# Loads of the next tile's keys and values issued a step ahead in a gated-delta recurrence, with their gate products behind the state sums

## The chip, the cores and the metric

The kernel runs on one core of a Trainium2 chip, in one launch. The metric is the device time of one execution in microseconds (us). Five engines work from queues of their own, each in the order in which its instructions stand: TensorE (PE, matmuls; its weight loads are shown as PEld), VectorE (DVE), ScalarE (ACT), GpSimd (POOL) and SyncE (SP). Transfers between the device's memory (DRAM) and the core's memory are issued from the queues of SP and ACT (shown as SPq and ACTq).

## The reference

A latent of 512 tokens by 1024 goes through two blocks beside a context of 256 tokens, all in float32. The change touches the first block's bidirectional gated-delta recurrence:

```
def gated_delta_chunked(q, k, v, g_log, beta, s0):
    # 8 heads of 64, chunks of 64 tokens
    ...
    w_mat = triangular_solve(t_mat, (bc * eG)[..., None] * kc, ...)
    u_v = triangular_solve(t_mat, bc[..., None] * vc, ...)
    k_tail = jnp.exp(g_last[..., None] - G)[..., None] * kc
    def step(S, xs):
        w_c, uv_c, qd_c, intra_c, kt_c, gl_c = xs
        u = uv_c - einsum('bhck,bhkv->bhcv', w_c, S)
        o = einsum('bhck,bhkv->bhcv', qd_c, S) + einsum('bhij,bhjv->bhiv', intra_c, u)
        S = exp(gl_c)[..., None, None] * S + einsum('bhck,bhcv->bhkv', kt_c, u)
        return S, o
```

It runs forwards and backwards, first over the context and then, from the states that this leaves, over the latent. `t_mat` is a triangular matrix of keys and gates for each chunk. The second block (two layers of attention, pooling and MLP) and the final norm aren't touched.

## The kernel before

The recurrence is `delta()`. Keys and values of the 768 tokens lie in DRAM as six tiles of 128 tokens by 512 (8 heads of 64), which makes 256 KB each. A **step** `s` (0 to 5) takes one tile for each direction `d`; steps 0 and 1 are the context, 2 to 5 the latent. A tile holds two chunks, which are the two **halves** `i` of a step. The steps go in three **groups** of two, and a group has three stages:

- `subst(g)` inverts 32x32 blocks of the triangular matrices on VectorE. A block copy on ScalarE (L959) and a transpose `Lw` (L960) come first, then 31 rounds of a product (L967) and a subtraction (L969), each needing the one before.
- `merges(g)` makes 64x64 inverses of them: two transposes on VectorE (L984 makes `Z2`, L985 `Z1`), matmuls (L993, L1003, L1006), and copies into the group's matrix on ScalarE (L1011 copies `Z2` and `Z1`, four instructions each; L997, L1014) and VectorE (L1015). The group's matrices take the buffer `M` that the stage before read.
- `chains(g)` carries the states through the two steps. A step makes `WT` from the gated keys `kb` (L1046 on PE, copied by ACT L1049), then `U` from the gated values `vc` (L1059). For each half, `U` takes up the state (L1072), ScalarE copies it to `u` (L1078), PE forms the state products `d` from the keys `kc` (L1092), and VectorE adds them to the decayed state (the **state sums**, L1102; the decay `Sg`, L1083). From step 2 on the outputs follow (L1112, L1116, copied by L1119 or summed by L1121), and for steps 4 and 5 `output()` (L1132 loads `sz`).

`fetch(s, d)` brings a tile: two loads that ScalarE's queue issues (L1027 keys, L1028 values) and at once the three gate products on VectorE (L1030, 128x512 each): `kb` is the keys by one gate, `vc` and `kc` are scaled in place. There are two buffers of each for each direction. Step `s+1` is fetched inside step `s`, once its `WT` stands, between the matmuls of `U`.

The group's substitution and merges run beside the chains of the group before it: `side_by_side` interleaves the generators and `weave` fills in work that doesn't depend on them. One filler is `attn_half()`, eight rounds of a weight load (L724, SP) that is split in two (ACT L728 `whi`, DVE L729 `wlo`), a gate load (L726, SP) for ACT's sigmoid (L730 `ga`), 12 matmuls (L447), a product on VectorE (L738) and a store from ScalarE's queue (L739). Its buffer `wst` is single. The other is `ada()`: weight loads on SP (L193) and matmuls (L201). These are interleaved as the code says, and then a scheduler in the compiler fixes the order on each engine (`schedule_with_timeline_sim=True`), so that a moved line can move others too.

## Time and profile before

| what | value |
|---|---|
| device time, median of 3 runs | 2660.58 us (2660.32, 2660.58, 2667.91) |
| the profiled execution's own time | 2655.62 us |
| its span (first to last instruction) | 2653.8 us |
| mean granted TensorE clock | 0.958 of full |
| instructions | 40142 |
| busy: TensorE, VectorE, ScalarE, GpSimd | 2469.4, 1486.5, 1004.2, 875.8 us |

The span is one execution as the hardware profiler saw it; 1.8 us of that execution lie outside it. The recurrence takes some 206 of the span's 2653.8 us, from about 456 to 662 us after its start. Times below are counted from the span's start. "Idle before" is how long an engine did nothing ahead of an instruction, with what ended that; the name behind it is inferred from semaphores.

### The profile page before, as it was taken

The numbers are of one execution on the slowest core, as the hardware profiler recorded it, in microseconds if no ns is written. First come the engines' busy times: TensorE is split into PE (matmuls) and PEld (weight loads), VectorE is DVE, ScalarE is ACT, GpSimd is POOL, SyncE is SP. The second block draws the span as 40 slices with busy tenths as digits, with TensorE's granted clock in tenths as the row PEclk, the third lists the DMA queues.
The fourth block names the chain that finished last, engine by engine and source line by source line (L and its number), as shares of the span: only waits on it lengthen the run. The fifth ranks groups of instructions, "written<-read, shape, count | busy, mean of one in ns | idle before, by whom it ended". The sixth has DMA issues, their size and how long they took to land.

```text
span 2653.8 us, 40142 instructions
## 1 busy us (share of the span) xinstructions
PE 2469.4 (93%) x16082; PEld 2097.0 (79%) x16082; DVE 1486.5 (56%) x2532; ACT 1004.2 (38%) x1824; POOL 875.8 (33%) x719
## 2 busy tenths in 40 slices
PE   6897997878999899999998999999998999999998
PEld 3886776556877778799787888888887987888888
DVE  4557658775479942352784887676227357522225
ACT  4545453432442232342663413121224265522332
POOL 2443101000742332455334523232235523523331
PEclk7998998788999999999999999999999999999999
DMA  7231164664535533310012253433212101233331
GB/s 258 74 101 44 56 188 153 219 221 163 179 107 183 167 119 99 100 63 25 9 52 92 94 159 117 126 125 116 64 64 66 44 17 64 85 97 99 96 106 48
DMA packets 249145, 282.53 MB, mean 106 GB/s; under 512 B 12168, under 2 KB 207359, under 8 KB 248703
## 3 DMA queue, kind: packets, MB, share of 16 engines
q1 hardware_dynamic: 225582, 249.86, 29.6%
q10 hardware_dynamic: 23376, 30.11, 3.4%
q8 instruction: 126, 2.06, 0.3%
q14 instruction: 61, 0.49, 0.1%
HBM read 264.06 MB, written 15.88 MB: 105 GB/s over the span
## 4 chain that ended last, share of the span: by engine, by line
PE 70%; DVE 15%; DMA 6%; ACT 4%; issue 3%; POOL 1%; SPq 0%; ACTq 0%; POOLq 0%; DVEq 0%
PE mm L447 60%; DMA wada<-in_w_ada_dram 3%; DVE aacc L242 2%; DVE nt L313 2%; PE sc L1825 2%; PE mm L1850 1%; DVE wlo L108 1%; PE mm L1859 1%; PE mm L1354 1%; DVE tmp L967 1%; ACT whi L435 1%; DVE X L969 1%; DMA ga<-sga 1%; DMA Gb<-grows 1%; PE mm L201 0%
## 5 line engine op out<-in xcount | busy, mean ns | idle before, releaser
L108 POOL TENSOR_TENSOR wlo<-wst,whi 128x1024 fp32r<-128x1024 f32 (+2 forms) x141 | 367.2, 2605 | 769.7 <-ACT whi L435 753.6
L435 ACT ACTIVATE whi<-wst 128x1024 fp32r<-128x1024 f32 (+2 forms) x293 | 287.9, 1031 | 636.4 <-PE mm L447 350.5
L447 PE MATMUL mm<-hmxl,whi 128*128 128x512 f32 (+1 forms) x816 | 314.3, 387 | 4.1 <-DVE hmxl L316 3.2
L447 PE MATMUL mm<-hmxh,whi 128*128 128x512 f32 (+1 forms) x816 | 310.8, 386 | 6.7 <-ACT hmxh L315 6.3
L447 PE MATMUL mm<-hmxh,wlo 128*128 128x512 f32 (+1 forms) x816 | 312.5, 385 | 2.5 <-DVE wlo L108 2.5
L447 PE MATMUL mm<-hidxl,whi 128*128 128x512 f32 (+1 forms) x720 | 280.6, 390 | 7.0 <-DVE hidxl L1478 7.0
L447 PE MATMUL mm<-hidxh,wlo 128*128 128x512 f32 (+1 forms) x720 | 279.9, 389 | 2.4 <-DVE wlo L108 2.4
L447 PE MATMUL mm<-hidxh,whi 128*128 128x512 f32 (+1 forms) x720 | 277.4, 388 | 0.0
L108 DVE TENSOR_TENSOR wlo<-wst,whi 128x1024 fp32r<-128x1024 f32 (+1 forms) x152 | 193.2, 1276 | 148.0 <-ACT whi L435 147.8
L242 DVE SCALAR_TENSOR_TENSOR aacc<-wada,silu,aacc 128x512 f32<-128x512 f32 x280 | 249.0, 937 | 26.0 <-DMA wada<-in_w_ada_dram 25.6
L329 DVE SCALAR_TENSOR_TENSOR xres<-mm,mod,xres 128x512 f32<-128x512 f32 (+1 forms) x122 | 85.0, 703 | 235.9 <-PE mm L447 235.7
L1474 POOL TENSOR_TENSOR nsq<-nt 128x512 f32<-128x512 f32 (+1 forms) x134 | 138.2, 1033 | 149.2 <-ACT nt L1473 127.7
L447 PEld LDWEIGHTS mm<-hmxh,whi 128*128 128x128 f32 x816 | 156.5, 194 | 37.3 <-ACT hmxh L315 7.3
L447 PEld LDWEIGHTS mm<-hmxl,whi 128*128 128x128 f32 x816 | 157.5, 193 | 35.5 <-DVE hmxl L316 4.8
L447 PEld LDWEIGHTS mm<-hmxh,wlo 128*128 128x128 f32 x816 | 157.5, 193 | 33.5 <-DVE wlo L108 3.7
L1478 DVE TENSOR_TENSOR hidxl<-nsq,hidxh 128x512 fp32r<-128x512 f32 (+1 forms) x102 | 75.8, 744 | 172.1 <-POOL nsq L1474 170.6
L447 PEld LDWEIGHTS mm<-hidxl,whi 128*128 128x128 f32 x720 | 136.2, 189 | 37.0 <-DVE hidxl L1478 9.4
L447 PEld LDWEIGHTS mm<-hidxh,wlo 128*128 128x128 f32 x720 | 136.1, 189 | 31.4 <-DVE wlo L108 3.2
L447 PEld LDWEIGHTS mm<-hidxh,whi 128*128 128x128 f32 x720 | 136.0, 189 | 27.8
L1473 ACT ACTIVATE nt<-mm 128x512 f32<-128x512 f32 (+1 forms) x134 | 69.5, 520 | 230.7 <-PE mm L447 224.7
L447 PE MATMUL mm<-whi,h2xh 128*128 128x256 f32 x384 | 110.4, 290 | 3.9 <-ACT raw L1608 2.6
L447 PE MATMUL mm<-wlo,h2xh 128*128 128x256 f32 x384 | 109.2, 287 | 0.0
(517 smaller groups left out, 6033.6 us busy)
## 6 DMA issues: line engine op xcount, KB each, us to landing
wst<-in_w_mlp_dram SPq DMA_DIRECT2D x96, 1024.0 KB, 5.5
wada<-in_w_ada_dram SPq DMA_DIRECT2D x160, 256.0 KB, 2.7
wst<-in_w_in_dram SPq DMA_DIRECT2D x35, 1024.0 KB, 5.4
wada<-in_w_ada_dram SPq DMA_DIRECT2D x48, 512.0 KB, 5.3
wst<-in_w_out_dram SPq DMA_DIRECT2D x10, 1024.0 KB, 7.0
wada<-in_w_ada_dram SPq DMA_DIRECT2D x8, 1024.0 KB, 13.7
xacc<-in_w_out_dram SPq DMA_DIRECT2D x16, 256.0 KB, 2.9
Gb<-grows SPq DMA_DIRECT2D x12, 256.0 KB, 4.2
```

The lines of the kernel that those rows point to most:

```text
L108: e.tensor_tensor(out, x, hi.bitcast(F32), ALU.subtract)
L242: nc.vector.scalar_tensor_tensor(acc[j], wt, c, acc[j], ALU.mult, ALU.add)
L313: nc.vector.scalar_tensor_tensor(t, x[:, k, :], a(k), self.rb[n], ALU.mult, ALU.mult)
L329: nc.vector.scalar_tensor_tensor(x[:, m, :], ps[:, :T], gate(m, n), x[:, m, :], ALU.mult, ALU.add)
L435: self.nc.scalar.activation(hi[:, :, c0:c1], st[:, :, c0:c1], AF.Copy)
L447: self.nc.tensor.matmul(ps, lhs[a](k), rhs[b](k), start=first and i == 0, stop=last and i == n - 1)
L967: nc.vector.tensor_tensor(t, Lw[:, j + 1:, j:j + 1].to_broadcast([P, n, w]), x[:, j:j + 1, 0:w].to_broadcast([P, n, w]), ALU.mult)
L969: nc.vector.tensor_tensor(x[:, j + 1:, 0:w], x[:, j + 1:, 0:w], t, ALU.subtract)
L1473: nc.scalar.activation(t, ps[:, :T], AF.Relu)
L1474: nc.gpsimd.tensor_tensor(s2, t, t, ALU.mult)
L1478: self.latest = nc.vector.tensor_tensor(lo, s2, hi.bitcast(F32), ALU.subtract)
L1825: mm = nc.tensor.matmul(ps[:, c0:c1], QT_[:, w, t * P:(t + 1) * P], KT_[:, c0:c1], start=w == 0, stop=w == 1)
```

## The change

`fetch` is split. It now only issues the two loads, and is called for step `s+1` at the start of step `s`, ahead of `WT`. A new `scale(s, d)` does the three gate products: for a group's first step ahead of the loop, and for step `s+1` direction by direction behind the state sums of the two halves of step `s`. No instruction is added or taken away on any engine. Line numbers behind this place grow by 7 to 11: the product is L1037, `WT` L1060, the `u` copy L1088, `Sg` L1093, the state sum L1112, the `oacc` copy L1130.

```diff
                 k, v, kb = (self.T(pool, [P, 8, CH], f"{n}{d}", bufs=2) for n in ("kc", "vc", "kb"))
                 nc.scalar.dma_start(out=k.rearrange("p h f -> p (h f)"), in_=tokd["k"][t])
                 nc.scalar.dma_start(out=v.rearrange("p h f -> p (h f)"), in_=tokd["v"][t])
+                loads[s, d] = [t, k, v, kb, False]
+
+            def scale(s, d):
+
+                if (s, d) not in loads or loads[s, d][4]:
+                    return
+                t, k, v, kb, _ = loads[s, d]
                 for x, y, f in ((kb, k, "nbg"), (v, v, "be"), (k, k, "ktl")):
                     nc.vector.tensor_tensor(x, y, dl[f][:, t, d, :].unsqueeze(2).to_broadcast([P, 8, CH]), ALU.mult)
-                loads[s, d] = t, k, v, kb
+                loads[s, d][4] = True
 
             both = range(2)
             for d in both:
                 fetch(2 * g, d)
+            for d in both:
+                scale(2 * g, d)
             for s in (2 * g, 2 * g + 1):
...
                 WT = [self.T(pool, [P, 4, P], f"WT{d}") for d in both]
+                for d in both:
+                    fetch(s + 1, d)
...
                 for d in both:
-                    fetch(s + 1, d)
                     v = loads[s, d][2]
...
                                     nc.vector.tensor_tensor(S1[e, :, e], Sg[d][e], pv[e], ALU.add)
+                    scale(s + 1, i)
                     yield
```

What the scheduler makes of it is seen in the order of each engine's rows. The first place is VectorE at the end of the second substitution (beside step 1). `X1_716` is that substitution's result, `Lw_831` the start of the third one; `kb0_794`, `kc0_792`, `kb1_803` and `kc1_801` are step 2's keys, `vc0_852` a value tile of step 3 (the digit behind the letters is the direction). Before:

```order
L969 TENSOR_TENSOR X1_716_4401<-X1_716_4401,tmp_717_4402 128x31
L984 STREAM_TRANSPOSE Z2_812_4996<-X1_716_4401 128x32x32
L985 STREAM_TRANSPOSE Z1_811_4995<-X1_716_4401 128x32x32
L1030 TENSOR_TENSOR kb0_794_4843<-kc0_792_4841,gnb_169_947 128x512
L1030 TENSOR_TENSOR kb1_803_4894<-kc1_801_4892,gnb_169_947 128x512
L729 TENSOR_TENSOR wlo_777_4748<-wst_774_4743,whi_776_4747 128x512
L738 TENSOR_TENSOR ga_761_4626<-mm0_784_4790,ga_761_4626 128x512
L1030 TENSOR_TENSOR kc0_792_4841<-kc0_792_4841,gktl_159_893 128x512
L1030 TENSOR_TENSOR kc1_801_4892<-kc1_801_4892,gktl_159_893 128x512
L1030 TENSOR_TENSOR vc0_852_5320<-vc0_852_5320,gbe_134_739 128x512
L960 STREAM_TRANSPOSE Lw_831_5227<-X1_834_5230 128x1024
```

After, on the same engine, where `kb1_786` and `kc1_784` belong to step 2 and `vc0_838` to step 3 (the names' numbers are new):

```order
L738 TENSOR_TENSOR ga_761_4620<-mm0_790_4800,ga_761_4620 128x512
L969 TENSOR_TENSOR X1_716_4401<-X1_716_4401,tmp_717_4402 128x4x28
L1037 TENSOR_TENSOR kb1_786_4769<-kc1_784_4767,gnb_169_947 128x512
L967 TENSOR_TENSOR tmp_717_4402<-Lw_715_4400,X1_716_4401 128x87
L1037 TENSOR_TENSOR kc1_784_4767<-kc1_784_4767,gktl_159_893 128x512
L969 TENSOR_TENSOR X1_716_4401<-X1_716_4401,tmp_717_4402 128x3x29
L967 TENSOR_TENSOR tmp_717_4402<-Lw_715_4400,X1_716_4401 128x60
L969 TENSOR_TENSOR X1_716_4401<-X1_716_4401,tmp_717_4402 128x2x30
L967 TENSOR_TENSOR tmp_717_4402<-Lw_715_4400,X1_716_4401 128x31
L969 TENSOR_TENSOR X1_716_4401<-X1_716_4401,tmp_717_4402 128x31
L1037 TENSOR_TENSOR vc0_838_5241<-vc0_838_5241,gbe_134_739 128x512
L984 STREAM_TRANSPOSE Z2_812_4993<-X1_716_4401 128x32x32
```

Step 2's four key products, one pair of L729 and L738 and the first of step 3's value products have moved from behind the two transposes to ahead of them (the first direction's two products and the L729 stand just above these rows). Behind L984 follow L985, the other value product, the next pair and `Lw`.

The second place is VectorE around the end of the third substitution, beside step 2, whose first state sums are `S01_709` and `S11_712` (two instructions each); `X0_832` is this substitution's result. Before:

```order
L967 TENSOR_TENSOR tmp_833_5229<-Lw_831_5227,X0_832_5228 128x135
L1102 TENSOR_TENSOR S01_709_4388<-Sg0_860_5403,d_863_5426 64x4x64 x2
L1102 TENSOR_TENSOR S11_712_4391<-Sg1_861_5407,d_864_5427 64x4x64 x2
L969 TENSOR_TENSOR X0_832_5228<-X0_832_5228,tmp_833_5229 128x5x27
L1083 TENSOR_TENSOR Sg0_870_5476<-S01_709_4388,gegs_160_895 64x256 x2
L1083 TENSOR_TENSOR Sg1_871_5480<-S11_712_4391,gegs_160_895 64x256 x2
```

After, with `vc1_887` a value product of step 4 (that of the other direction stands ten rows above it):

```order
L969 TENSOR_TENSOR X0_832_5228<-X0_832_5228,tmp_833_5229 128x31
L984 STREAM_TRANSPOSE Z2_920_5880<-X0_832_5228 128x32x32
L985 STREAM_TRANSPOSE Z1_919_5879<-X0_832_5228 128x32x32
L1037 TENSOR_TENSOR vc1_887_5618<-vc1_887_5618,gbe_134_739 128x512
L729 TENSOR_TENSOR wlo_852_5319<-wst_849_5314,whi_851_5318 128x512
L738 TENSOR_TENSOR ga_817_5039<-mm0_858_5353,ga_817_5039 128x512
L1112 TENSOR_TENSOR S01_709_4388<-Sg0_860_5397,d_863_5420 64x4x64 x2
L1112 TENSOR_TENSOR S11_712_4391<-Sg1_861_5401,d_864_5421 64x4x64 x2
L1093 TENSOR_TENSOR Sg0_870_5473<-S01_709_4388,gegs_160_895 64x256 x2
L1093 TENSOR_TENSOR Sg1_871_5477<-S11_712_4391,gegs_160_895 64x256 x2
L729 TENSOR_TENSOR wlo_868_5450<-wst_865_5445,whi_867_5449 128x512
L738 TENSOR_TENSOR ga_850_5315<-mm0_873_5488,ga_850_5315 128x512
```

Step 2's state work stood from the 27th of the 31 rounds on, and now all stands behind the last round and the two transposes. From the `Lw` of the third substitution up to the end of L985, VectorE has 12 state instructions, three pairs of L729 and L738 and two gate products fewer.

The third place is ScalarE in the same stretch. `u1_850` (after: `u0_855` and `u1_856`) is step 2's, `kc0_892` and `kc1_899` (after: `kc0_883`, `kc1_886`) are step 4's keys, `Z2_920` and `Z1_919` the third substitution's transposes. Before:

```order
L1078 ACTIVATE u1_850_5318<-u_848_5316 64x512
L1027 DMA kc0_892_5687<-tok_k_98_448 128x512
L730 ACTIVATE ga_866_5449<-ga_866_5449 128x512
L739 DMA sga_101_451<-ga_844_5305 128x512
L1027 DMA kc1_899_5728<-tok_k_98_448 128x512
L1011 ACTIVATE M1_583_3283<-Z2_920_5880 32x2x8x32 x4
L1119 ACTIVATE oacc_707_4383<-mm1_877_5540 128x512
L1011 ACTIVATE M1_583_3283<-Z1_919_5879 32x2x8x32 x4
```

After:

```order
L1011 ACTIVATE M1_583_3283<-Z2_920_5880 32x2x8x32
L1011 ACTIVATE M1_583_3283<-Z1_919_5879 32x2x8x32 x4
L1088 ACTIVATE u0_855_5327<-u_853_5325 64x512
L1088 ACTIVATE u1_856_5328<-u_854_5326 64x512
L739 DMA sga_101_451<-ga_817_5039 128x512
L728 ACTIVATE whi_867_5449<-wst_865_5445 128x512
L1088 ACTIVATE u0_855_5327<-u_853_5325 64x512
L1088 ACTIVATE u1_856_5328<-u_854_5326 64x512
L730 ACTIVATE ga_866_5446<-ga_866_5446 128x512
L1027 DMA kc0_883_5612<-tok_k_98_448 128x512
L739 DMA sga_101_451<-ga_850_5315 128x512
L1027 DMA kc1_886_5617<-tok_k_98_448 128x512
```

The copies of the transposes stood behind step 2's four `u` copies and now stand ahead of them, the second half's `u` copies have an L728 ahead of them, and the first load of step 4's keys has moved behind an L730. TensorE's order is nearly the same as before, and from step 3's first state sums on VectorE and ScalarE have the same rows in nearly the same order too.

## Rows read from the trace of the kernel before

**Rows 1.** The page: busy time by engine, and the chain that ended last by engine.
```profile
PE 2469.4 (93%) x16082; PEld 2097.0 (79%) x16082; DVE 1486.5 (56%) x2532; ACT 1004.2 (38%) x1824; POOL 875.8 (33%) x719
...
PE 70%; DVE 15%; DMA 6%; ACT 4%; issue 3%; POOL 1%; SPq 0%; ACTq 0%; POOLq 0%; DVEq 0%
```

**Rows 2.** Three windows: us, then busy PE PEld DVE ACT POOL, PEclk, DMA share, GB/s.
```profile
456.50:510.50 54.00, 38.70 (x616) 26.58 (x616) 46.05 (x106) 20.35 (x35) 2.79 (x6) 0.69 0.66 218
510.50:524.00 13.50, 12.63 (x211) 7.94 (x210) 7.96 (x9) 10.96 (x16) 0.00 (x0) 1.00 0.86 273
524.00:573.30 49.30, 38.79 (x680) 28.08 (x682) 43.21 (x108) 13.55 (x27) 1.03 (x2) 0.83 0.65 204
```

**Rows 3.** VectorE's waits, 440 to 662 us: total us, times, longest.
```profile
DVE vc L1030 <- DMA vc<-tok_v: 14.0, 5, 5.5
DVE S L1102 <- PE d L1092: 13.8, 6, 4.2
...
DVE kb L1030 <- DMA kc<-tok_k: 2.9, 2, 1.9
```

**Rows 4.** ScalarE's waits, same stretch and columns.
```profile
ACT ga L730 <- DMA ga<-sga: 19.7, 5, 5.7
```

**Rows 5.** VectorE's timeline: start, us, instruction, xcount [idle before it <-what ended it].
```profile
510.38 2.03 DVE L984 STREAM_TRANSPOSE Z<-X 128x1024 f32<-128x1024 f32 x1
...
514.13 1.25 DVE L1030 TENSOR_TENSOR kb<-kc,gnb 128x512 f32<-128x512 f32 x2
...
523.42 0.69 DVE L1030 TENSOR_TENSOR vc<-vc,gbe 128x512 f32<-128x512 f32 x1 [5.51 <-DMA vc<-tok_v]
524.03 1.92 DVE L960 STREAM_TRANSPOSE Lw<-X 128x1024 f32<-128x1024 f32 x1
```

**Rows 6.** ScalarE's timeline, same place (ACTq is a transfer being issued).
```profile
506.05 0.33 ACTq L1027 DMA_DIRECT2D kc<-tok_k  x1
...
516.62 2.55 ACT L1011 ACTIVATE M<-Z 32x512 f32<-32x512 f32 x4
518.56 0.33 ACTq L1028 DMA_DIRECT2D vc<-tok_v  x1
...
519.19 1.06 ACT L959 ACTIVATE X<-M 32x1024 f32<-32x1024 f32 x1
...
520.26 3.19 ACT L959 ACTIVATE X<-M 32x1024 f32<-32x1024 f32 x3
```

**Rows 7.** TensorE's timeline, step 2, state products.
```profile
562.37 0.97 PE L1092 MATMUL d<-u,kc 64*64 64x64 f32 x32
```

**Rows 8.** VectorE's timeline, from step 2 to step 3.
```profile
558.57 0.69 DVE L1030 TENSOR_TENSOR vc<-vc,gbe 128x512 f32<-128x512 f32 x1 [2.37 <-DMA vc<-tok_v]
...
566.28 1.72 DVE L1102 TENSOR_TENSOR S<-Sg,d 64x256 f32<-64x256 f32 x4
...
576.99 2.10 DVE L985 STREAM_TRANSPOSE Z<-X 128x1024 f32<-128x1024 f32 x1
...
584.99 0.69 DVE L738 TENSOR_TENSOR ga<-mm,ga 128x512 f32<-128x512 f32 x1 [1.83 <-issue]
...
596.46 1.73 DVE L1102 TENSOR_TENSOR S<-Sg,d 64x256 f32<-64x256 f32 x4
```

**Rows 9.** ScalarE's timeline, load of step 4's keys.
```profile
571.85 0.33 ACTq L1027 DMA_DIRECT2D kc<-tok_k  x1
```

**Rows 10.** Transfers of the whole span: count, size, median us to landing.
```profile
kc<-tok_k ACTq DMA_DIRECT2D x12, 256.0 KB, 4.8
vc<-tok_v ACTq DMA_DIRECT2D x12, 256.0 KB, 3.6
...
wst<-in_w_br_attn_dram SPq DMA_DIRECT2D x8, 256.0 KB, 3.1
ga<-sga SPq DMA_DIRECT2D x8, 256.0 KB, 3.3
sga<-ga ACTq DMA_DIRECT2D x8, 256.0 KB, 4.7
```

## The prediction, made before the changed kernel ran

> **What bounds the kernel now.** I read the page first. TensorE is busy 93% of the span and holds 70% of the chain that ended last, VectorE 15% [rows 1], so the question is whether the recurrence is one of the places where TensorE runs dry. The windows answer it. In the two substitution stretches beside the chains (456.5 to 510.5 and 524 to 573.3 us) VectorE is busy 46.05 of 54.0 and 43.21 of 49.3 us, TensorE 38.7 and 38.79, at a granted clock of 0.69 and 0.83 of full. Only in the 13.5 us between them is TensorE full (12.63 us, clock 1.00) [rows 2]. So here VectorE's queue and the chain through it set the pace. Outside the recurrence nothing changes its place, and what moves there moves as a whole.
>
> Next, what VectorE waits for. Value products wait 14.0 us in five places for their loads, key products 2.9 in two, and state sums 13.8 in six for TensorE [rows 3]. The first two are what the change is about. VectorE takes its rows in their order, so a product that waits for its load stops the substitution behind it. ScalarE, which issues these loads, itself waits 19.7 us in its sigmoid L730 for the gate load of the filler [rows 4]: a load that stands behind that row starts late, whatever its own place in the code.
>
> Third, which of the five waits cost anything. The longest, 5.51 us, ends at 523.42, and `Lw` starts right behind it at 524.03 [rows 5]. But `Lw` also reads the block copies L959 of ScalarE, the last of which ends at 520.26 + 3.19 = 523.45 [rows 6]. So that wait is covered by the copies. The next (2.37 us, at 558.57 [rows 8]) stops a substitution in the middle, with nothing beside it.
>
> **The change, step by step.** No work is added; what counts is where rows stand. I walked VectorE's and ScalarE's new rows and took each duration from a row of before, in five pivots.
>
> *1. Start of the third substitution.* Ahead of the transpose L984 now stand four key products, a pair L729 and L738, and one value product. Two products took 1.25 us [rows 5], so 0.63 each; L738 took 0.69 [rows 8] and I take 1.4 for the pair: 4 x 0.63 + 1.4 + 0.63 = 4.5 us. The value product may wait, since its load is issued behind the store of the same pair's result, some 2.8 us of VectorE rows ahead. The load lands in 3.6 us in the median [rows 10]; with the longest wait of before, 5.5 us [rows 3], and 1.8 of the 2.8 us running meanwhile, I bound the wait by 0 and 3.7. L984 before started at 510.38 [rows 5], now between 514.9 and 518.6. Behind it ScalarE's chain is unchanged: half of the 3.75 us from L984 to the next product [rows 5], twice 2.55 us for L1011, and 523.45 - 519.19 = 4.26 us for L959 [rows 6], in all 11.3 us. `Lw` starts between 526.2 and 529.9; I take the middle, 528.0. Before: 524.03. That is 4 us lost.
>
> *2. The third substitution to the end of L985.* Before: 576.99 + 2.10 [rows 8] - 524.03 = 55.1 us. Moved behind it are 12 state instructions of 0.43 us (four took 1.72 [rows 8]), or 5.2; three pairs, 4.2; two products, 1.3; and the 2.37 us wait goes. 55.1 - 5.2 - 4.2 - 1.3 - 2.4 = 42.0 us. A new wait comes in: step 4's first value load stands behind an L730, and VectorE's rows reach its product ten rows before L985's end. Bounds 0 and 4.5 (of the longest L730 wait, 5.7 [rows 4], less 1.2 for the rows that run meanwhile); I take the 2.4 of the same product before. L985 ends at 528.0 + 42.0 + 2.4 = 572.4, where it ended at 579.1: 6.7 us early.
>
> *3. Step 2's first state sums.* They now stand behind all this. ScalarE copies Z1 (2.55), then `u` (two at 0.6, 1.2 us), TensorE forms `d` (0.97 [rows 7]): 577.1. On VectorE a value product and a pair come first (2.0 us from 572.4, hidden unless the load is late); I take 577.4. Before: 566.28 [rows 8]. The state chain is 11.1 us late, and its cover, the substitution, has gone.
>
> *4. Step 2's second half.* Its `u` copies stand behind an L728, which needs a weight load that SP can issue only when L729 has freed the buffer (VectorE's row just ahead of L738, about 576.5). With 3.1 us to land [rows 10] and 0.6 for L728, `u` comes at about 581.4, `d` at 582.4 and its sums, behind another pair, at 584.6.
>
> *5. Step 3's first state sums.* Step 4's key load was issued at 571.85 [rows 9]. It now stands behind an L730, whose gate load SP holds back until the store of pivot 3's L738, which ended at about 577.0, has landed. 577.0 + 4.7 for the store + 3.3 for the load [rows 10] + 0.6 for L730 = 585.6; the keys land 4.8 us later [rows 10], at 590.7 with issuing. Four key products (2.5) and L738 (0.7) follow and end at about 594.5, where before that L738 ended at 585.68 [rows 8]. From there to the sums VectorE took 10.8 us before (to 596.46 [rows 8]), 5.4 of it in waits for a value load and a sigmoid; part of these is over by then, and I count 8.0. Sums at 602.5, against 596.46: **6 us late**. From here on the rows stand in nearly the old order, and TensorE's fill behind them keeps its place, so the shift goes to the end.
>
> **Sum.** Against before, `Lw` is 4 us late, L985's end 6.7 early, step 2's first state sums 11.1 late and step 3's 6 late; the last goes to the end. On the profiled execution 2655.62 + 6 = 2661.6. That one lies 5.0 us under the median of the runs shown, 2660.58, so on the median 2666.6. With both waits of pivots 1 and 2 at zero (-4.3) and the 3.7 us of rest waits in pivot 5 gone the sum is -2; with them at their upper ends (+4.0), and 1 us more at the L728, it is +11. The forecast's own range is 2658.6 to 2671.6.
>
> A rule of the Trainium skill speaks against the whole of the change: the page "Perfetto Trace Analysis", section "Optimization Strategy", says that a gap repeating for a stretch can mean that there is no buffer space for the next tile. In the trace step 2's key load goes out at 506.05 [rows 6], when the state sums of step 0, which used that buffer, are past; so for the keys the trace agrees, and an earlier call can't start them earlier. By that rule alone the time would be that of rival B.
>
> **Rivals.**
> *B, nothing reaches the end:* the late sums and the early substitution cancel, 2660.6, within 2. For it: 5.51 of the 14.0 us were covered by ScalarE's copies, and TensorE has fill to do in most gaps. Against: pivot 5's chain of store, load, sigmoid and keys has no cover in the rows.
>
> *C, faster:* the third group's matrix counts, not step 2's sums. If step 3 can wait for its state while the third merges run early, the 6.7 us of pivot 2 stay. If the value waits of 14.0 and key waits of 2.9 [rows 3] go altogether, it is 16.9. Midway: 11.8 off, 2648.8. It decides from step 3's sums at 588.5 on, 8 us ahead of before [rows 8]. Against: in TensorE's order the third merge's matmuls still stand behind step 3's state product, which needs pivot 4's sums.
> The Trainium skill has this as a rule ("DMA: Bandwidth & Descriptors", section "Rules for kernel authors": issue the transfer early, compute, wait late); by it the 14.0 us would go, and the time would be 2646.6. The wait that ended at 523.42 speaks against the whole of that.
>
> *D, clearly slower:* the value product ahead of L984, and the one ten rows ahead of L985's end, find their loads late as the worst of before. Each wait is then 5.5 us [rows 3] in place of my 1.9 and 2.4: +6.7 on top of the 6, so 2673.3. From 2 us over my two waits on, the result is slower by more than the bound below. For it: both loads are issued behind rows of ScalarE that wait for other transfers [rows 4]; and the DMA share in the stretch is 0.65 to 0.86 [rows 2].
>
> **How the numbers follow.** Chances: forecast 0.53, B 0.18, C 0.13, D 0.16. A measurement tells 0.3%, or 8 us, from no change (the three runs lie 7.6 us apart). The forecast's +6 in -2 to +11 lies over +8 in some 4 of 10 cases: 0.21 slower, 0.32 same. B is same. C, between 6.7 and 16.9 us off, gives 0.11 faster and 0.02 same; D is slower. Sum: faster 0.11, same 0.52, slower 0.37. The range leaves out most of C (0.12) and half of D (0.08): 2654 to 2673.
>
> **What would show it.** Right: VectorE's `Lw` (L960) at about 528, L985 ending near 572, step 2's first state sums (now L1112) near 577 instead of 566, step 4's key load issued near 586 behind L730, step 3's sums near 602, and the end 6 us late. The five value waits should shrink, with one or two new ones ahead of L984 and L985, and the waits of L1112 for TensorE should grow. Wrong: if the sums at step 3 are not later than 597, pivot 5 has failed; if `Lw` isn't late, pivot 1; if the shift at 662 us is not found at the span's end, TensorE's fill took it up.

## The result, and the profile after

The changed kernel takes 2681.23 us (median of 4 runs, 2680.08 to 2683.5) where the kernel before, beside it, took 2660.45: a ratio of 1.0078 (95% interval 1.0065 to 1.009). It is 20.8 us slower, by more than the whole range foresaw. Its profiled execution took 2680.08 us with a span of 2678.3, 24.5 over that of before; the profiled execution of before is a quick one (2655.62 us), so what follows adds up to more than 20.8.

The page of the changed kernel, busy time and chain by engine, in answer to [rows 1]:

```profile
PE 2474.6 (92%) x16082; PEld 2101.8 (78%) x16082; DVE 1486.3 (55%) x2532; ACT 1005.2 (38%) x1824; POOL 872.6 (33%) x719
...
PE 72%; DVE 14%; DMA 6%; ACT 4%; issue 3%; POOL 1%; ACTq 0%; SPq 0%; POOLq 0%; DVEq 0%
```

The instructions and VectorE's busy time (1486.3 for 1486.5 us) are those of before: nothing was added, so the time must be in waits. The windows of the recurrence, with the columns of [rows 2]:

```profile
456.50:516.40 59.90, 43.96 (x756) 30.42 (x756) 49.83 (x114) 21.65 (x38) 3.69 (x8) 0.75 0.72 232
516.40:532.70 16.30, 4.77 (x104) 3.03 (x100) 6.08 (x8) 9.89 (x14) 0.00 (x0) 0.74 0.72 243
532.70:576.60 43.90, 33.63 (x504) 22.68 (x504) 39.10 (x92) 12.19 (x24) 1.03 (x2) 0.69 0.42 129
576.60:593.00 16.40, 12.33 (x164) 9.01 (x164) 8.25 (x18) 7.13 (x13) 0.00 (x0) 0.72 0.54 173
593.00:615.30 22.30, 18.60 (x374) 13.19 (x366) 8.61 (x18) 6.08 (x12) 0.00 (x0) 0.95 0.83 261
```

The second line is the stretch between the second and the third substitution. Before, TensorE was busy 12.63 of its 13.5 us at full clock [rows 2]; now it is busy 4.77 of 16.3, VectorE 6.08. Both engines wait. The last row of the recurrence on VectorE starts at 686.93, where it was 662.71; from there to the span's end it is 1991.4 us, and was 1991.1. A few rows behind the recurrence have changed their place too, against what the prediction says, but as a whole that stretch takes as long as before. The recurrence's first L984 starts at 458.26, where it was 457.41, so 0.85 us of the 24.2 arise ahead of it (in the runs below it starts between 456.97 and 461.54); the rest lies in the recurrence. The pivots of the prediction show where it grows. The last column is what a link added to the error of the forecast:

| pivot | before | predicted | measured | error added |
|---|---|---|---|---|
| 1: `Lw` starts | 524.03 | 528.0 | 532.67 | +4.7 |
| 2: L985 ends | 579.09 | 572.4 | 576.64 | -0.4 |
| 3: step 2's first sums | 566.28 | 577.4 | 581.83 | +0.2 |
| 4: step 2's second sums end | 576.96 | 584.6 | 593.01 | +4.0 |
| 5: step 3's first sums | 596.46 | 602.5 | 615.25 | +4.3 |
| last row of the recurrence | 662.71 | 668.7 | 686.93 | +5.4 |

**The first place.** VectorE's timeline ahead of the third substitution:

```profile
510.95 0.69 DVE L1037 TENSOR_TENSOR kb<-kc,gnb 128x512 f32<-128x512 f32 x1 [1.65 <-DMA kc<-tok_k]
...
516.24 0.19 DVE L969 TENSOR_TENSOR X<-X,tmp 128x31 f32<-128x31 f32 x1
520.73 0.69 DVE L1037 TENSOR_TENSOR vc<-vc,gbe 128x512 f32<-128x512 f32 x1 [4.30 <-PE mm L201]
521.34 1.91 DVE L984 STREAM_TRANSPOSE Z<-X 128x1024 f32<-128x1024 f32 x1
...
532.67 1.95 DVE L960 STREAM_TRANSPOSE Lw<-X 128x1024 f32<-128x1024 f32 x1 [5.92 <-ACT X L959]
```

The second substitution is ready at 516.43; L984 could start there and starts at 521.34, since a value product of step 3 stands ahead of it and its load is late. (The row puts the wait down to TensorE's L201, of which the product reads nothing; the chain of the profile has the value load there, issued at 514.21 and 6.43 us long.) With a key wait of 1.65 us two loads hold up the queue. ScalarE's timeline, same place:

```profile
511.18 0.63 ACT L730 ACTIVATE ga<-ga 128x512 f32<-128x512 f32 x1 [2.17 <-DMA ga<-sga]
...
513.79 0.33 ACTq L739 DMA_DIRECT2D sga<-ga  x1
514.21 1.21 ACTq L1028 DMA_DIRECT2D vc<-tok_v  x1
...
523.28 5.10 ACT L1011 ACTIVATE M<-Z 32x512 f32<-32x512 f32 x8 [5.28 <-DVE Z L984]
...
531.59 1.05 ACT L959 ACTIVATE X<-M 32x1024 f32<-32x1024 f32 x1
532.67 1.21 ACT L1088 ACTIVATE u<-u 64x512 f32<-64x512 f32 x2
```

The value load goes out at 514.21, behind a sigmoid that waited and behind the filler's store, which waits for VectorE's L738; it lands 6.4 us later. The late L984 pushes the rest of the chain with it: step 1's `u` copies stand behind all of L1011 and L959, as they did before, and start at 532.67 for 524.00. TensorE's timeline shows what that does. Before, its state products of step 1:

```profile
524.63 0.68 PE L1092 MATMUL d<-u,kc 64*64 64x64 f32 x16 [1.21 <-ACT u L1078]
```

After, here and at the second place:

```profile
533.31 1.74 PE L1102 MATMUL d<-u,kc 64*64 64x64 f32 x32 [8.62 <-ACT u L1088]
...
580.67 1.18 PE L1102 MATMUL d<-u,kc 64*64 64x64 f32 x20 [7.42 <-ACT u L1088]
```

TensorE runs dry for 8.62 and 7.42 us; before it waited 1.21 us at the first place and didn't wait for `u` at the second [rows 7].

**The second place.** VectorE from the end of the third substitution, in answer to [rows 8]:

```profile
572.95 1.92 DVE L984 STREAM_TRANSPOSE Z<-X 128x1024 f32<-128x1024 f32 x1
574.77 1.87 DVE L985 STREAM_TRANSPOSE Z<-X 128x1024 f32<-128x1024 f32 x1
577.73 0.69 DVE L1037 TENSOR_TENSOR vc<-vc,gbe 128x512 f32<-128x512 f32 x1 [1.09 <-DMA vc<-tok_v]
...
581.83 1.73 DVE L1112 TENSOR_TENSOR S<-Sg,d 64x256 f32<-64x256 f32 x4 [2.21 <-PE d L1102]
...
589.92 0.69 DVE L729 TENSOR_TENSOR wlo<-wst,whi 128x512 fp32r<-128x512 f32 x1 [4.54 <-ACT ga L730]
...
591.25 1.76 DVE L1112 TENSOR_TENSOR S<-Sg,d 64x256 f32<-64x256 f32 x4
...
602.72 0.69 DVE L738 TENSOR_TENSOR ga<-mm,ga 128x512 f32<-128x512 f32 x1 [3.83 <-PE mm L447]
...
609.33 0.69 DVE L1037 TENSOR_TENSOR vc<-vc,gbe 128x512 f32<-128x512 f32 x1 [3.83 <-DMA vc<-tok_v]
...
613.25 1.48 DVE L1145 TENSOR_TENSOR sz<-sz,O 128x512 f32<-128x512 f32 x2 [2.88 <-ACT O L1144]
...
615.25 1.73 DVE L1112 TENSOR_TENSOR S<-Sg,d 64x256 f32<-64x256 f32 x4
```

The state sums stand behind both transposes and wait for `u` as well. The sums of step 2's second half stand behind an L729 that waits 4.54 us, but `u` and the state products are no earlier than that. TensorE and ScalarE, same stretch:

```profile
586.55 1.58 PE L1082 MATMUL u<-S,WT 128*64 128x128 f32 x16
...
587.67 1.21 ACT L1088 ACTIVATE u<-u 64x512 f32<-64x512 f32 x2 [4.58 <-PE u L1082]
```

The weight load has come (L728 runs at 582.46), and the `u` copies then wait 4.58 us for TensorE's L1082, which takes up the state behind eight of the filler's matmuls (L447, 583.43 to 586.62). After its 7.42 us of idleness TensorE runs at the lower of its two clock levels for a while (granted clock 0.50 from 580.6 to 583.4 and 0.63 from there to 586.6 us; before, 1.00 in these rows), so the eight take 3.19 us, where they took 2.14. The last of these state products ends at 590.96, 0.3 us ahead of the sums at 591.25. Step 3's sums stand behind the filler's next product, a value product and two `sz` products, and all of these wait.

**The third place** was not foreseen. VectorE between step 4's last sums and step 5's first:

```profile
646.28 0.85 DVE L1112 TENSOR_TENSOR S<-Sg,d 64x256 f32<-64x256 f32 x2 [1.33 <-PE d L1102]
647.16 0.69 DVE L1132 TENSOR_TENSOR oacc<-oacc,mm 128x512 f32<-128x512 f32 x1
...
651.36 0.69 DVE L1153 TENSOR_TENSOR O<-oacc,dr 128x512 f32<-128x512 f32 x1 [1.83 <-POOL dr L1152]
651.97 0.68 DVE L1132 TENSOR_TENSOR oacc<-oacc,mm 128x512 f32<-128x512 f32 x1
...
655.98 0.69 DVE L1153 TENSOR_TENSOR O<-oacc,dr 128x512 f32<-128x512 f32 x1 [1.75 <-POOL dr L1152]
...
666.05 0.85 DVE L1112 TENSOR_TENSOR S<-Sg,d 64x256 f32<-64x256 f32 x2 [2.07 <-PE d L1102]
```

Before, the same rows with their old line numbers:

```profile
628.12 0.85 DVE L1102 TENSOR_TENSOR S<-Sg,d 64x256 f32<-64x256 f32 x2 [1.33 <-PE d L1092]
...
631.08 0.68 DVE L1121 TENSOR_TENSOR oacc<-oacc,mm 128x512 f32<-128x512 f32 x1
...
633.67 0.69 DVE L1142 TENSOR_TENSOR O<-oacc,dr 128x512 f32<-128x512 f32 x1 [0.32 <-POOL dr L1141]
...
642.83 0.85 DVE L1102 TENSOR_TENSOR S<-Sg,d 64x256 f32<-64x256 f32 x2 [0.54 <-PE d L1092]
```

The outputs of the two directions now run one behind the other: the second L1132 stands behind the first L1153, which waits for GpSimd. From sums to sums it takes 19.8 us; before, with both L1121 ahead of the first L1142, it took 14.7.

### The profile page after: what moved, and what is told of

It reads as the page before. It is cut to its first block, busy times and chain, and to the rows that moved or that the text cites. A ratio compares the mean times of both kernels' runs of the same rounds, so it can differ in the third digit from the quotient of the medians.

```text
span 2678.3 us, 40148 instructions
## 1 busy us (share of the span) xinstructions
PE 2474.6 (92%) x16082; PEld 2101.8 (78%) x16082; DVE 1486.3 (55%) x2532; ACT 1005.2 (38%) x1824; POOL 872.6 (33%) x719
## 4 chain that ended last, share of the span: by engine, by line
PE 72%; DVE 14%; DMA 6%; ACT 4%; issue 3%; POOL 1%; ACTq 0%; SPq 0%; POOLq 0%; DVEq 0%
PE mm L447 61%; DMA wada<-in_w_ada_dram 3%; DVE aacc L242 2%; PE sc L1836 2%; DVE nt L313 2%; PE mm L1861 2%; DVE wlo L108 1%; PE mm L1870 1%; PE mm L1365 1%; PE mm L201 1%; PE u L1082 1%; ACT whi L435 1%; DMA Gb<-grows 1%; DMA lamv<-in_lam_k_dram 0%; DVE X L969 0%
## 5 line engine op out<-in xcount | busy, mean ns | idle before, releaser
L447 PE MATMUL mm<-hmxl,whi 128*128 128x512 f32 (+1 forms) x816 | 314.9, 387 | 5.1 <-POOL hmxl L321 2.6
L447 PE MATMUL mm<-hmxh,whi 128*128 128x512 f32 (+1 forms) x816 | 310.7, 386 | 6.1 <-ACT hmxh L315 6.1
L447 PE MATMUL mm<-hmxh,wlo 128*128 128x512 f32 (+1 forms) x816 | 312.7, 385 | 2.6 <-DVE wlo L108 2.6
L447 PE MATMUL mm<-hidxl,whi 128*128 128x512 f32 (+1 forms) x720 | 279.7, 388 | 8.6 <-DVE hidxl L1489 8.6
L447 PE MATMUL mm<-hidxh,wlo 128*128 128x512 f32 (+1 forms) x720 | 279.0, 388 | 2.3 <-DVE wlo L108 2.3
L447 PE MATMUL mm<-hidxh,whi 128*128 128x512 f32 (+1 forms) x720 | 276.4, 387 | 0.0
L447 PEld LDWEIGHTS mm<-hmxl,whi 128*128 128x128 f32 x816 | 158.2, 194 | 36.4 <-DVE hmxl L316 3.8
L447 PEld LDWEIGHTS mm<-hmxh,whi 128*128 128x128 f32 x816 | 157.0, 194 | 36.8 <-ACT hmxh L315 7.1
L447 PEld LDWEIGHTS mm<-hmxh,wlo 128*128 128x128 f32 x816 | 158.3, 194 | 33.4 <-DVE wlo L108 3.8
L447 PEld LDWEIGHTS mm<-hidxl,whi 128*128 128x128 f32 x720 | 135.7, 188 | 38.7 <-DVE hidxl L1489 11.1
L447 PEld LDWEIGHTS mm<-hidxh,wlo 128*128 128x128 f32 x720 | 135.7, 188 | 31.2 <-DVE wlo L108 3.2
L447 PEld LDWEIGHTS mm<-hidxh,whi 128*128 128x128 f32 x720 | 135.6, 188 | 27.9
L447 PE MATMUL mm<-whi,h2xh 128*128 128x256 f32 x384 | 110.3, 290 | 3.1 <-ACT raw L1619 2.6
L447 PE MATMUL mm<-wlo,h2xh 128*128 128x256 f32 x384 | 109.5, 287 | 0.0
## 6 DMA issues: line engine op xcount, KB each, us to landing
wada<-in_w_ada_dram SPq DMA_DIRECT2D x8, 1024.0 KB, 14.3
```

What stands on the lines that cost most here:

```text
L447: self.nc.tensor.matmul(ps, lhs[a](k), rhs[b](k), start=first and i == 0, stop=last and i == n - 1)
```

## The experiments

Each kernel is one of the two with a short edit. `issue_after(x)` pins an instruction behind `x` in the scheduler's order. Nothing of the computation is left out in any of them. Ratios are to the kernel before, whose median lay between 2660.5 and 2662.7 us in these comparisons; differences between experiments are of medians that were taken beside different runs of it, so a difference of 2 us says little.

**1 and 2. Which half of the change does it?** Both kernels have `fetch` split as in the change. The first calls `fetch` ahead of `WT` and the products where they were; the second calls the loads where they were and the products behind the state sums:

```diff
+                for d in both:
+                    fetch(s + 1, d)
...
                 for d in both:
-                    fetch(s + 1, d)
+                    scale(s + 1, d)
```

```diff
                 for d in both:
                     fetch(s + 1, d)
...
+                    scale(s + 1, i)
                     yield
```

> Only the loads are called early; the three products are called where they were, inside the matmuls of U. Theory A (the scheduler places a product by when its load could have landed, so the place of scale() in the code does nothing and the early load call does all of it): the same rows as the changed kernel on every engine, 2681 us, within 4. Rival (the products behind the state sums cost part of it): at least 5 us less than the changed kernel, 2676 or below.

> Only the products are called late; the loads are called where they were. Theory A: the rows of the kernel before, 2660.5 us, within 3. Rival (late products cost part of it): 2666 or more.

Early loads alone: 2682.17, ratio 1.0069 (1.0049 to 1.009). Late products alone: 2661.13, 0.9996 (0.9985 to 1.0008). VectorE's rows in the first stand in the order of the changed kernel, in the second in that of before. So the second half of the change is inert, and the early load alone brings the products ahead of L984. That fits a scheduler that places a product by its own reckoning of when the load is there; how it reckons was not looked at.

**3. The first place undone.** The changed kernel with the products of steps 2 and 3 pinned behind the second substitution's transposes (`zt` is L985's instruction; step 2's are called at the group's start):

```diff
+                with ExitStack() as c:
+                    if s in (2, 3):
+                        c.enter_context(self.tc.issue_after(self.zt.ins))
+                    for x, y, f in ((kb, k, "nbg"), (v, v, "be"), (k, k, "ktl")):
```

> The changed kernel, early loads kept, with the products of steps 2 and 3 made to stand on VectorE behind the second substitution's transposes L984 and L985, as before the change. The third substitution's order goes back by itself (step 2's state sums stand inside it). Theory A (the loss comes from the order: products with their late loads ahead of L984, and what follows from it): L984 back at about 511, Lw (L960) at 524 to 526, the time 2660 us, between 2655 and 2664. Rival B (the early loads cost by themselves, by crowding the transfers or ScalarE's queue): still 2672 or more.

2656.64, ratio 0.9982 (0.9966 to 0.9998): 24.6 us come back with the loads still early, as theory A (`Lw` comes 1.3 us later than it said). Its VectorE timeline:

```profile
511.26 2.01 DVE L984 STREAM_TRANSPOSE Z<-X 128x1024 f32<-128x1024 f32 x1
...
527.28 1.97 DVE L960 STREAM_TRANSPOSE Lw<-X 128x1024 f32<-128x1024 f32 x1
...
557.33 0.84 DVE L1115 TENSOR_TENSOR S<-Sg,d 64x256 f32<-64x256 f32 x2
...
582.00 1.92 DVE L984 STREAM_TRANSPOSE Z<-X 128x1024 f32<-128x1024 f32 x1
...
591.17 1.73 DVE L1115 TENSOR_TENSOR S<-Sg,d 64x256 f32<-64x256 f32 x4 [1.89 <-PE d L1105]
```

Step 2's sums stand ahead of the third substitution's L984 again, though no pin touches them, and come at 557.33 (before 566.28 [rows 8]). The first place is the trigger: with it goes the second. That the early loads themselves cost time, by crowding other transfers, has no loss left to explain. The third place is still there (20.0 us from sums to sums).

**4. The second place undone alone.** The third substitution's transposes pinned behind step 2's second state sums:

```diff
+                if g == 2:
+                    c.enter_context(self.tc.issue_after(self.ss[2, 1].ins))
                 nc.vector.transpose(Z2.rearrange("a p c -> a c p"), x.rearrange("a r c -> a c r"))
```

> The changed kernel, where only the third substitution's transposes are made to stand behind step 2's state sums on VectorE; so the copies of the transposes stand behind step 2's u copies on ScalarE. The second substitution's end stays as in the changed kernel. Theory A (two places, each with a price): Lw stays at about 532.7, TensorE's wait for u of 7.4 us at step 2 goes, step 2's first state sums come at 573 to 576 instead of 581.8, and 8 to 12 us of the 21 come back: 2669 to 2673. Rival C (the second place only waits for the first, and its order is free): 2679 or more. Rival D (the whole loss is at the second place): 2663 or less.

2666.88, ratio 1.0023 (1.0012 to 1.0034): 14.3 us less than the changed kernel, more than theory A's 8 to 12 and less than rival D needs. First sums 572.42 (for 581.83), the recurrence's last row 673.64 (for 686.93), and TensorE's wait of 7.4 us is gone. Of these 13.3 us 2.6 are an earlier L984 at the first place (518.74), which the pin does not touch; that leaves about 11 for the second place.

**5. Is it ScalarE's order or VectorE's?** Only ScalarE's copies of `Z2` and `Z1` (L1011) of the third group pinned behind step 2's `u` copies; VectorE's order is that of the change:

```diff
+                        with ExitStack() as c:
+                            if g == 2:
+                                c.enter_context(self.tc.issue_after(self.uc[2, 1].ins))
```

> The changed kernel, with ScalarE's eight copies of Z2 and Z1 (L1011) of the third group pinned behind the u copies of step 2's second half; VectorE's order stays that of the changed kernel. It tells what made step 2's state sums late. Theory S (ScalarE's order: the u copies stand behind the block copies, which wait for VectorE's two transposes): the u copies run early, TensorE forms d and the sums' wait for it goes, but the sums still stand behind both transposes, so only the 5 us between L985's end and the sums come back, and step 2's second half follows; 2669 to 2676. Theory V (VectorE's order alone decides, since the sums stand behind the transposes of the third substitution whatever ScalarE does): the first sums at 577 to 580 for 581.8, the third merges late by the copies, and the time 2676 to 2684. Pinning the transposes behind the sums gave 2666.9.

2673.07, ratio 1.0043 (1.003 to 1.0057), as theory S. VectorE's timeline:

```profile
573.56 1.87 DVE L985 STREAM_TRANSPOSE Z<-X 128x1024 f32<-128x1024 f32 x1
...
577.06 1.72 DVE L1116 TENSOR_TENSOR S<-Sg,d 64x256 f32<-64x256 f32 x4
...
586.29 1.76 DVE L1116 TENSOR_TENSOR S<-Sg,d 64x256 f32<-64x256 f32 x4
```

The first sums come 1.6 us behind L985's end (573.56 + 1.87) in place of 5.2 and wait for nothing. So ScalarE's order counts, but for less than the 8.2 us between the medians: step 2's first sums come 4.8 us earlier than in the changed kernel and step 3's 5.0, and 2.3 of that is again an earlier L984 at the first place. The rest of the gain arises later, behind step 3's sums and behind the recurrence, where the pin has moved rows on VectorE too. At step 2's first sums ScalarE's order alone is thus worth some 2.5 us; in experiment 4 they came 9.4 us earlier, with 2.6 of that at the first place.

**6. Step 3's values too.** As 4, with step 3's value products behind the second substitution's transposes:

```diff
+                        if s == 3 and f == "be":
+                            c.enter_context(self.tc.issue_after(self.zt.ins))
```

> The kernel with the third substitution's transposes behind step 2's state sums (2666.9 us), and step 3's two value products moved behind the second substitution's transposes; the key products and the filler's pair still stand ahead of them. Theory A (of what is left at the first place, the wait of 4.2 us for the value load is most): L984 comes at 514 instead of 518.7, Lw at 525.5 instead of 530.1, and the time falls by 4 to 5 us, to 2662. Rival F (Lw isn't on the path any more, or the wait moves to the next row): 2665.5 or more.

2671.23, ratio 1.0032 (1.0019 to 1.0046): no gain over 4. `Lw` comes some 4 us earlier, counted from the section's start, but the next value product now stops the substitution for 4.16 us (for 2.69) and TensorE waits 6.52 behind it (for 1.27). Here the wait moved on with the product, as rival F.

**7. The third place.** The changed kernel with one more yield in `output()` and step 4's first L1153 pinned behind the other direction's L1151:

```diff
+            yield
+            with ExitStack() as c:
+                if i == 0 and s == 4:
+                    c.enter_context(self.tc.issue_after(self.dr[1].ins))
```

> The changed kernel, with one thing put back: at the outputs of step 4 VectorE takes both directions' sums and reductions ahead of the first product that waits for GpSimd, as before the change. Theory A (a third place: the outputs of step 4 run one after the other, 19.8 us from step 4's last state sums to step 5's first, where it was 14.7): that stretch is back at 14 to 15.5 us and the time falls by 5 us, to 2676, between 2674 and 2678. Rival E (it is covered by TensorE's work): 2679 or more.

2671.36, ratio 1.0039 (1.0025 to 1.0053), 9.9 us less, twice what theory A said. Step 4's sums to step 5's are 16.0 us (19.8 before the edit), the recurrence ends 4.5 us earlier; the other half of the gain falls behind the recurrence (1986.7 us from its last row to the span's end, for 1991.4), where the edit moves rows too. What does it there stays open.

**8. The second and third place together**, the edits of 4 and 7:

> The changed kernel with two pins at once: the third substitution's transposes behind step 2's state sums (alone 2666.9, 14.3 us off the changed kernel), and step 4's first output product behind the other direction's reduction (alone 2671.4, 9.9 off). Theory A (the two places are links of one chain and their losses add): 2681.2 - 14.3 - 9.9 = 2657, between 2654 and 2660. Theory B (each gives TensorE's fill a slot and they overlap): 2661 to 2667, no more than 5 us under the first pin alone.

2669.69, ratio 1.0033 (1.0022 to 1.0044): theory A is wrong, and so is the sum of single gains; the time lies above theory B's range too. The traces show two reasons. What 7 gained behind the recurrence isn't found here (1991.1 us, 1989.7 in 4). And the first place is dearer again. ScalarE's timeline in 4, and then in this kernel:

```profile
508.52 0.63 ACT L730 ACTIVATE ga<-ga 128x512 f32<-128x512 f32 x1 [1.29 <-DMA ga<-sga]
...
511.05 0.39 ACTq L1032 DMA_DIRECT2D vc<-tok_v  x1
```

```profile
512.84 0.63 ACT L730 ACTIVATE ga<-ga 128x512 f32<-128x512 f32 x1 [5.26 <-DMA ga<-sga]
...
515.87 0.39 ACTq L1033 DMA_DIRECT2D vc<-tok_v  x1
```

With the same order here, the gate load took 6.35 us from issue to landing for 3.00, the value load went out 4.8 us later, and L984 started at 522.58 for 518.74 (1.7 of these 3.8 us because the recurrence started later). The price of the first place is not fixed: it follows how long a transfer takes.

**9. First and third place undone**, the edits of 3 and 7, and **10.** the same with the products of steps 2 to 5 all pinned:

> The early loads kept, with the products of steps 2 and 3 behind the second substitution's transposes and the outputs of step 4 paired: both known places put back. Theory A: 2656.6 less 5, that is 2651.5, between 2648 and 2654, faster than the kernel before by some 9 us. Rival E: 2656 or more.

> Early loads, every gate product of steps 2 to 5 pinned behind both transposes of its substitution, and step 4's outputs in pairs. The same with only the products of steps 2 and 3 pinned gave 2649.0. Theory: with the second substitution's place in order the third place reverts by itself, so pinning it too changes nothing: 2647 to 2652. Rival: a pin that the order did not need takes rows out of gaps, and the products of steps 4 and 5 come late for WT: 2653 to 2660.

2648.96, ratio 0.9951 (0.9937 to 0.9966), and 2647.62, 0.9949 (0.9936 to 0.9962), as theory A and as the theory of 10: both faster than either kernel. In the profiles the recurrence, from its first L984 to its last row, takes 200.3 and 196.5 us, where it took 205.3 before and 228.7 in the changed kernel. **11.** Is that the early loads, or the edit of the outputs? The edit of 7 on the kernel before:

> The kernel before with the edit of the output rows that was made to the changed kernel (one more yield in output(), and step 4's first output product pinned behind the other direction's reduction). In the recurrence of before these rows already stand in that order, but the edit also moves rows of the attention that follows. Theory E (the early loads are worth time once their products stand late): this kernel does not get to 2649.0, the time with the early loads, late products and the same edit; 2655 to 2661. Theory N (the early loads bring nothing, and the edit moved the rows behind the section to a better order): 2646 to 2652.

2662.3, ratio 1.0 (0.9991 to 1.0009), as theory E, 1.3 us above its range. So the edit brings nothing by itself; with early loads and late products 9 is 13 us faster than this kernel. These go together with a new order of VectorE's rows from the second L984 on, which the scheduler chose; no run parts the earlier landing from that order.

**12. No product on VectorE.** The kernel before with its 36 gate products on GpSimd (`nc.gpsimd.tensor_tensor`):

> The kernel before, with all 36 gate products on GpSimd in place of VectorE, so that a late load stops no substitution. Theory A (a product in VectorE's queue is the harm, wherever it stands): the 14.0 and 2.9 us of load waits leave VectorE, with 36 products of 0.63 us; not all of it is on the path, so 2645 to 2655. Rival G (the products then reach TensorE late: GpSimd took 1.03 us for a product of this shape, with three per direction and step): 2660 or more.

2650.95, ratio 0.9956 (0.9939 to 0.9972), inside theory A's range, although a product takes 1.1 us there for 0.69. But only part of that is the recurrence: in the profiles it takes 203.6 us for 205.3, and the stretch behind it 1987.6 for 1991.1. There rows have moved as well, so the load waits that left VectorE explain the smaller part. **13.** The changed kernel with the same edit and that of 7, and **14.** with the pin of 4 as well:

> The changed kernel with all 36 gate products on GpSimd in place of VectorE, and step 4's outputs in pairs. Theory F (the early loads lost time only because their products stood in VectorE's row order ahead of the transposes; on a queue with nothing behind them a late load stops nobody): 2640 to 2650, at or under the kernel before with its products on GpSimd (2651.0). Rival G (GpSimd's product is slower, and WT and the state products of TensorE wait for it; the early loads themselves bring nothing): 2650 to 2660.

> The changed kernel with all gate products on GpSimd, step 4's outputs in pairs, and the third substitution's transposes pinned behind step 2's state sums. Without that pin it took 2661.0, with no product of the change left on VectorE, and there step 2's sums still stood behind the transposes and waited 4.0 us for TensorE. Theory 2 (the place of the sums costs time by itself, with no product and no value load in it): the first sums at 561 to 565 for 570.4, and the time 2648 to 2654. Rival (the transposes that start 6.5 us earlier than in the kernel before with GpSimd's products were worth as much as the late sums cost): within 3 of 2661.

2660.99, ratio 0.9996 (0.9985 to 1.0007), and 2648.59, 0.9959 (0.9945 to 0.9974). Theory F is wrong, and the time lies above rival G's range as well: in 13 the third substitution doesn't start late (`Lw` at 518.70, at 521.03 in 12), and yet the kernel is 10 us over 12. VectorE's timeline in 13, and then in 14:

```profile
563.24 1.87 DVE L985 STREAM_TRANSPOSE Z<-X 128x1024 f32<-128x1024 f32 x1
...
570.39 1.74 DVE L1113 TENSOR_TENSOR S<-Sg,d 64x256 f32<-64x256 f32 x4 [4.03 <-PE d L1103]
```

```profile
562.79 1.72 DVE L1117 TENSOR_TENSOR S<-Sg,d 64x256 f32<-64x256 f32 x4
...
571.73 1.97 DVE L987 STREAM_TRANSPOSE Z<-X 128x1024 f32<-128x1024 f32 x1
```

As theory 2: with no product and no value load in it, the second place costs 12.4 us by itself; TensorE waits 9.1 us for `u` in 13, which stands behind L1011. With that put right the early loads gain nothing that can be told from 12 (0.9959 for 0.9956).

## Why the prediction was wrong

The forecast's sign of each pivot was right, and the chance of slower stood at 0.37, below the 0.52 of no change; the size was wrong by 18.2 us on the profiled executions (+24.2 at the end of the recurrence for +6). Nearly all of it lies in four terms that were too small or missing. The steps in turn:

*Pivot 1 failed in its size* (4.7). "The value product may wait", bounded by 0 and 3.7 with 1.9 taken: measured 4.30, and a key wait of 1.65 that the step gave nothing. The bound let 1.8 us run while the load was on its way, from a store 2.8 us ahead of L984; in the trace the load went out 1.1 us behind the start of that store's L738, at 514.21, and took 6.4 us, longer than the 5.5 taken as the worst. Rival D had this mechanism, at +6.7. The chain behind L984 was right (11.3 us to `Lw`, predicted and measured); that the same chain holds step 1's `u` copies, so that TensorE runs dry for 8.62 us, stands in none of the cases. Experiment 3 shows that this place decides.

*Pivot 2 was right as a stretch:* from `Lw` to L985's end 43.97 us, predicted 44.4, with a value wait of 2.30 for 2.4; since `Lw` was late, 2.5 us were won and not 6.7. *Pivot 3 was right as a step:* the first sums come 5.2 us behind L985's end, predicted 5.0. "The state chain is late, and its cover, the substitution, has gone" is what experiments 4 and 14 show; their price of 11 to 12 us is about what the step gave (11.1).

*Pivot 4 failed.* It put the second half's delay at the weight load and gave TensorE's take-up of the state (L1082) nothing. The weight load was not what `u` waited for: TensorE took up the state behind eight matmuls of the filler, which the lower clock made 1 us longer, and the copies waited 4.58 us for that. On VectorE L729 waits 4.54 us in the same stretch: its buffer `wlo` is single, and the filler's matmuls L447 read it until 589.83. Both chains reach the sums within 0.3 us of each other, so neither alone is the price. Adds 4.0, where the 584.6 of the step is read as the end of the sums.

*Pivot 5 failed.* Its chain does not run through pivot 4 but starts at pivot 3's L738, which ended at 579.62 for 577.0. Step 4's key load went out at 590.48, predicted 586, and the keys landed at 595.37, predicted 590.7. Behind the four key products the next L738 waited 3.83 us for the filler's matmuls, which the step gave nothing, and ended at 603.41 for 594.5 (0.6 of the 594.5 is in none of the step's own terms: 590.7 + 2.5 + 0.7 is 593.9). "Part of these is over by then, and I count 8.0": it took 11.8, none of the rest waits had gone. The value product waits 3.83 and the `sz` products 2.88, since their loads (ScalarE's queue, 604.21, and SP, 605.26) had slipped with everything else. Against the chain of sums this adds 4.3.

*"From here on the rows stand in nearly the old order" was wrong.* Step 4's outputs stand in series, a term that the forecast put at nothing; experiment 7 has this at 4 to 5 us in the recurrence. Adds 5.4. "The shift goes to the end" was right: 1991.4 us remain, for 1991.1.

Two smaller slips: the lower end of the range takes 3.7 us of rest waits out of pivot 5, which had only 2.6 left (8.0 of 10.8, with 5.4 of waits); and at 506.05 the state products of step 0 are past, not its sums (506.55). Of the signs that were to show a right forecast, the value waits did not shrink (15.0 us in five places, the one put down to L201 among them, for 14.0), and the sums' waits for TensorE did grow (17.8 for 13.8).

Rival B, that gains and losses cancel, fell with the result. Rival C's time is what experiments 9 and 10 reach, but not by its mechanism. The waits for values are not gone there (14.0 us in six places in 9; 14.0 in five before [rows 3]), and the third group's matrix does not count: in 9 `Lw` starts at 529.82, 5.8 us later than before, and L985 ends at 588.47, 9.4 later, yet step 2's first sums come at 559.49, 6.8 earlier, and step 3's at 593.75, 2.7 earlier. So the state chain is the path there, and the substitution has slack: what pivot 2 wins has no worth of its own. The gain lies between step 1's last sums and step 2's first, 17.5 us in 9 (541.96 to 559.49) for 28.1 before (538.22 to 566.28). Which link of that stretch gives it, and whether it is the early landing or the new order, is not settled. By the Trainium skill ("DMA: Bandwidth & Descriptors", section "Rules for kernel authors": issue early, wait late) the change should have been faster; the runs agree only where the wait too is late (0.9951), and with the load alone moved the ratio is 1.0069. The other rule of the Trainium skill ("Perfetto Trace Analysis", section "Optimization Strategy": a gap that repeats can mean that there is no buffer for the next tile) fits the keys: step 2's went out at 506.47, before at 506.05 [rows 6].

The chain of single edits, in medians: 2681.2 with all three places, 2666.9 without the second, 2656.6 without first and second, 2649.0 without any. These steps (14.3, 10.2, 7.7) depend on the order in which they are taken, as experiments 7 and 8 show. Of the last, the profiles have 2.5 us in the recurrence (202.8 to 200.3) and 2.0 behind it, which are not explained.

## What to carry to other kernels

An earlier load can be an earlier consumer where a scheduler chooses the consumer's place: here the call of the load moved the products, and their own call did not. Look at what stands behind the consumer in its engine's queue, and pin it behind the work that must not wait. When a stretch is a chain of queues, price a late row by every engine behind it: here two load waits of together 6 us on VectorE and the products moved ahead of L984 raised TensorE's wait for `u` from 1.2 to 8.6 us, by way of ScalarE's copies. And follow the new order to the end of the section: "nearly the old order" was 5 us.

## What the runs showed that was not expected

- Same order, other transfer times: in experiments 4 and 8 one gate load (256 KB) let L730 wait 1.29 and 5.26 us, and the first place moved by 2.2 us, counted from the recurrence's first L984.
- The kernel is 0.44% faster with the 36 products on the slower engine (1.1 us each on GpSimd, 0.69 on VectorE). Of 3.8 us between the profiled executions 3.6 lie behind the recurrence, though, and why is open.
